# A bidirectional gated scan: the two halves of a head's outputs change places

## The chip, the core and the metric

The kernel runs on one core of one Trainium2 chip. The core has engines that run side by side, each through its own list of instructions in order: TensorE (PE in the profile; its weight loads are PEld), VectorE (DVE), ScalarE (ACT), GpSimd (POOL) and SyncE (SP), which issues most of the DMAs. They meet through semaphores. The metric is the device time of one execution in microseconds (us), the median of the runs.

## What is computed

One layer of an encoder over 1024 positions of width 1024. A normed input is projected by one wide matrix; part of the result goes through a convolution module, part through a bidirectional linear recurrence with 8 heads of width 128, and both are gated and merged; a feed-forward network with a short convolution follows. The change concerns the recurrence (`_bi_hgrn2`). Per head and direction:

```python
# S_t = diag(f_t) S_{t-1} + k_t v_t^T,  o_t = S_t^T q_t
o_fwd = _chunk_gated_scan(qh, heads(k_f), vh, heads(lf_f))
flip = lambda t: jnp.flip(t, axis=1)
o_bwd = flip(_chunk_gated_scan(flip(qh), flip(heads(k_b)), flip(vh), flip(heads(lf_b))))
return o_fwd + o_bwd
...
of = o * lax.rsqrt(jnp.mean(o * o, axis=-1, keepdims=True) + EPS)
of = of.reshape(o.shape[0], o.shape[1], HGRN_WIDTH) * norm_w.astype(jnp.float32)
bmix = (of * jax.nn.silu(og.astype(jnp.float32))).astype(h.dtype)
```

So the outputs of a position need a forward state, summed from the left, and a backward state, summed from the right.

## The kernel before

The kernel keeps TensorE supplied through four stages: the projection, the scan of the heads, the merge, and the feed-forward network. Most products are made of three matmuls in a split format (lines 150 to 152, `mm3`). TensorE's order is the order of the program text (`manual_schedule`). On the other engines a planner orders the instructions by what is ready and by their place in the text, except where the text pins them.

**The scan stage.** The sequence of 1024 is two halves of 512; a half is four chunks of 128. The loop at line 1493 runs over the 8 heads and, inside, over the halves; step `i = 2h + half`. Each step has five places, numbered 0 to 4, at which `between(n)` puts in other work: dense matmuls of the remaining projection columns and of the convolution module (`dense.fill(FILL)`, 1.77 pieces on average, a piece being two of a job's k-steps, six matmuls), then one piece of the previous head's outputs (`pending.fill(1)`), then a step of a base that is prepared ahead (`ahead` at places 0 to 3, `following` at place 4). A head's outputs are therefore made while the first half of the next head is under way, and its final scaling and transposes while the second half is.

**What a step makes.** `scan_base` (line 1241) doubles keys and queries level by level on VectorE, with interleaving copies on ScalarE; its pages are `kG` (3 buffers) and `qF` (4 buffers). `scan_levels` (line 1294) makes a score matrix per chunk: it copies it to `S` and lets GpSimd patch the diagonal blocks by four DMAs (line 1343). `scan_states` (line 1346) transposes the keys (line 1354) and makes the state updates: the forward states `Sf` are chained on VectorE at once (lines 1370 and 1372); the backward ones are only copied, to `Sb` (lines 1382 and 1384), since they need the chunks to their right.

**What the outputs make.** `outputs` (line 1459) first chains the backward states on VectorE, six dependent instructions for chunks 5, 4, 3, 2, 1, 0 (line 1463); chunks 4 to 7 are the second half, in the tile `Sb[1]`, chunks 0 to 3 the first, in `Sb[0]`. After a `yield`, that is one place later, `scan_outputs` (line 1387) makes a half's outputs: per chunk up to three matmuls (line 1405) into the PSUM bank `ob`, of which there is one, then ScalarE copies the bank to a page `on` (line 1407), takes four sums of squares (line 1410), and SP loads the gate (line 1415). One more place later comes the other half, and then the statistic `rs` for both on GpSimd (lines 576 and 577). In the places after that ScalarE scales the two halves (line 1424), and TensorE transposes them for VectorE to gate (line 1434).

A chunk's matmuls read `S`, `v`, the half's `qF` page, `Sf` of the chunk and `Sb` of the chunk. Pages with few buffers are handed on: the base of step `i + 4` takes the `qF` page of step `i`. For the last head there is no next head to run beside; there the places are spelled out (`TAIL`, lines 1528 to 1530), with one dense piece between the two halves' outputs.

Of the kernel before, what the change touches and what calls it, by code (L numbers as in the profile page):

```python
# [49 lines left out]
def tile_hybrid_encoder(  # L50
# [45 lines left out]
    def nm(s):  # L96
        uid[0] += 1
        return f"{s}_{uid[0]}"
# [3 lines left out]
    def bank(tag):  # L102
        return ps.tile([P, H], F32, tag=tag, name=nm(tag), bufs=BANKS[tag])

    def page(pool, tag, bufs, dt=F32):
        return pool.tile([P, H], dt, tag=tag, name=nm(tag), bufs=bufs)

    def tmp():
        return page(mp, "tm", 4)

    def ev():
        return page(mp, "ev", 3)

    def hx():
        return page(mp, "hx", 32, F32R)
# [9 lines left out]
    def split(hi, lo, src, eng, late=False):  # L125
        parts = A.copy(hi, src), eng.tensor_tensor(lo, src, hi.bitcast(F32), op=ALU.subtract)  # L126
        if late:
            for i in parts:
                pin(i)
        return hi, lo  # L130
# [399 lines left out]
    def vec(key, i):  # L530
        name, o = vec_off[key]
        return vecs[name][:, o + i : o + i + 1]
# [41 lines left out]
    def rstd_small(dst, ss, n, late=False):  # L574
        hold = pin if late else lambda i: i
        hold(G.tensor_scalar(dst, ss, 1.0 / n, EPS, op0=ALU.mult, op1=ALU.add))
        hold(G.tensor_tensor(dst, dst, mhalf.to_broadcast(list(dst.shape)), op=ALU.pow))
# [583 lines left out]
    hp = tc.alloc_tile_pool(name="heads", bufs=1, reuse_waits="tile")  # L1161
# [225 lines left out]
    def scan_outputs(h, kept, Sf, Sb):  # L1387


        ons, gates = [], []  # L1390
        ss = cp.tile([P, 2, 4], F32, name=nm("oss"), tag="oss", bufs=2)
        rs = cp.tile([P, 2, 4], F32, name=nm("ors"), tag="ors", bufs=2)
        for half in range(2):
            S_t, v, qF = kept[half]
            o = bank("ob")
            for c in range(4):
                sl = slice(c * P, (c + 1) * P)
                g = half * 4 + c
                terms = [(S_t[:, c, :], v[:, c, :])]
                if g > 0:  # L1400
                    terms.append((qF[:, 1, sl], Sf[half][:, c, :]))
                if g < 7:
                    terms.append((qF[:, 0, sl], Sb[half][:, c, :]))
                for n, (l, r) in enumerate(terms):
                    T.matmul(o[:, sl], l, r, start=(n == 0), stop=(n == len(terms) - 1))  # L1405
            on = tmp()
            A.copy(on, o)
            for c in range(4):
                junk = hp.tile([P, DK], F32, tag="jk", name=nm("jk"), bufs=1)
                A.activation(  # L1410
                    junk, on[:, c * P : (c + 1) * P], AF.Square, accum_out=ss[:, half, c : c + 1]
                )
            ons.append(on)
            gates.append(page(hp, "og", 2))
            nc.sync.dma_start(gates[half], d_og[h][half])
            if half == 0:
                yield
        rstd_small(rs, ss, DK)
        yield
        yield  # L1420
        for half in range(2):
            for c in range(4):
                sl = slice(c * P, (c + 1) * P)
                done = A.activation(
                    ons[half][:, sl], ons[half][:, sl], AF.Copy, scale=rs[:, half, c : c + 1]
                )
            last_scaled[:] = [done]
            yield
        for half in range(2):
            b = bank("tr")  # L1430
            for c in range(4):
                T.transpose(b[:, c * P : (c + 1) * P], ons[half][:, c * P : (c + 1) * P], ident)
            bt = ev()
            V.scalar_tensor_tensor(bt, b, vec("hn", h), gates[half], op0=ALU.mult, op1=ALU.mult)
            if h == NH - 1:
                bm[h][half] = split(hx(), hx(), bt, V)
            else:
                nc.sync.dma_start(d_bm[h][half], bt)
            yield
# [19 lines left out]
    def outputs(h, kept, Tt, Sf, Sb):  # L1459
        for c in range(5, -1, -1):  # L1460
            hf, cc = c // 4, c % 4
            n1, c1 = (c + 1) // 4, (c + 1) % 4
            V.scalar_tensor_tensor(
                Sb[hf][:, cc, :],
                Sb[n1][:, c1, :],
                Tt[:, n1, 1, c1 : c1 + 1],
                Sb[hf][:, cc, :],
                op0=ALU.mult,
                op1=ALU.add,
            )  # L1470
        yield
        yield from scan_outputs(h, kept, Sf, Sb)
# [626 lines left out]
```

## Time and profile before

| | |
|---|---|
| median of 3 runs | 1715.56 us |
| lowest and highest | 1714.04 and 1716.18 us |
| the profiled execution | 1714.14 us |
| its span, first to last instruction | 1712.0 us |
| mean granted TensorE clock | 0.998 |

A row of a view of groups has the line, the engine, the operation and the tiles written and read, then the count and times. A row of a timeline has the start in us from the start of the span, the duration in us, then the engine, line, operation, tiles and shapes; `x2` says that two instructions were merged, and brackets hold the time that the engine stood idle before and what ended it. A row of waits says which engine waited at which line, for which line of which engine, and for how long in total, how often, and at most. The scan lies between about 505 and 860 us of the span. In these stretches, one per head, the engines' busy time in us (windows of the trace; heads' outputs are made in the stretch after their own):

```text
555.00:599.00 44.00, 42.23 (x698) 36.14 (x697) 37.19 (x81) 32.35 (x75) 6.28 (x10) 1.00 0.44 137
599.00:642.00 43.00, 43.00 (x702) 37.11 (x701) 36.55 (x78) 32.89 (x76) 6.51 (x10) 1.00 0.40 128
642.00:686.00 44.00, 43.45 (x702) 37.20 (x700) 37.90 (x85) 32.12 (x75) 6.29 (x10) 1.00 0.42 130
```

The columns are the stretch, its length, then PE, PEld, DVE, ACT and POOL with their counts, the granted clock, the share of the DMA engines and GB/s.

### The profile page before, as it was taken

The page shows a single profiled execution, that of the slowest core. Times are in us where ns is not written, and L with a number is a line of the kernel's source. Part 1 is how long each engine was busy: PE and PEld are TensorE (multiplying, and loading weights), DVE is VectorE, ACT ScalarE, POOL GpSimd, SP SyncE. Part 2 cuts the span into 40 slices and gives each one's busy share as a digit, 9 for nine tenths or more (in the row PEclk, how much of TensorE's full clock was granted, in tenths as well). Part 3 has the DMA queues.
Part 4 walks back from the last instruction along what each step waited for, and adds up shares of the span by engine and source line. Part 5 has one row for each costly group of instructions (what it writes and reads, how often), then busy time and mean ns, then how long its engine had stood idle before and what let it go on. Part 6 is the DMA issues. An engine that isn't in the chain of part 4 may idle for free.

```text
span 1712.0 us, 30393 instructions
## 1 busy us (share of the span) xinstructions
PE 1691.4 (99%) x11719; PEld 1407.6 (82%) x11719; DVE 1263.8 (74%) x1938; ACT 826.2 (48%) x1562; POOL 241.9 (14%) x281
## 2 busy tenths in 40 slices
PE   8999999999999999999999999999999999999998
PEld 6788888888888888888888888888888888888787
DVE  5899999545778888888656467677777776657865
ACT  7444343334666777776432245444344434542334
POOL 1312222200001111111100002122222222000110
PEclk9999999999999999999999999999999999999999
DMA  7887888854673444436788355677777776773852
GB/s 240 279 215 181 191 195 197 208 157 143 223 242 100 137 128 134 128 116 214 233 280 260 123 172 178 151 163 154 166 164 176 171 173 150 236 264 100 214 98 99
DMA packets 332870, 306.16 MB, mean 179 GB/s; under 512 B 17454, under 2 KB 244918, under 8 KB 332726
## 3 DMA queue, kind: packets, MB, share of 16 engines
q1 hardware_dynamic: 285366, 265.42, 48.5%
q0 software_dynamic: 47360, 38.81, 15.5%
q8 instruction: 92, 1.51, 0.4%
q14 instruction: 52, 0.43, 0.1%
HBM read 201.40 MB, written 84.93 MB: 167 GB/s over the span
## 4 chain that ended last, share of the span: by engine, by line
PE 87%; DVE 4%; ACT 2%; DMA 2%; issue 1%; SPq 0%; POOL 0%; POOLq 0%; ACTq 0%; DVEq 0%
PE mm L150 20%; PE mm L152 19%; PE mm L151 19%; PE sc L150 5%; PE sc L151 5%; PE sc L152 5%; PE tr L150 2%; PE tr L151 2%; PE tr L152 2%; PE ob L1405 2%; PE sc L1219 1%; DVE qF L1166 1%; DVE kG L1166 1%; PE sc L1364 1%; PE mm L1364 1%
## 5 line engine op out<-in xcount | busy, mean ns | idle before, releaser
L150 PE MATMUL mm<-hx,wp 128*128 128x512 f32 x1068 | 426.0, 399 | 0.5 <-DVE ev L825 0.4
L152 PE MATMUL mm<-hx,wp 128*128 128x512 f32 x1068 | 417.1, 391 | 0.5 <-DVE wp L126 0.5
L151 PE MATMUL mm<-hx,wp 128*128 128x512 f32 x1068 | 416.2, 390 | 0.6 <-POOL hx L126 0.6
L126 ACT CAST wp<-wr 128x1024 fp32r<-128x1024 f32 (+2 forms) x146 | 146.7, 1005 | 210.6 <-PE mm L151 160.8
L152 PEld LDWEIGHTS mm<-hx,wp 128*128 128x128 f32 x1068 | 200.5, 188 | 44.8 <-DVE wp L126 1.6
L150 PEld LDWEIGHTS mm<-hx,wp 128*128 128x128 f32 x1068 | 200.5, 188 | 42.4 <-DVE ev L825 2.0
L151 PEld LDWEIGHTS mm<-hx,wp 128*128 128x128 f32 x1068 | 200.8, 188 | 39.9 <-POOL hx L126 1.0
L126 DVE TENSOR_TENSOR wp<-wr,wp 128x1024 fp32r<-128x1024 f32 (+2 forms) x144 | 169.4, 1177 | 34.8 <-ACT wp L126 34.5
L1061 DVE SCALAR_TENSOR_TENSOR acc<-gl,v_b,acc 128x1024 f32<-128x1024 f32 x120 | 148.7, 1275 | 0.3
L442 ACT COPY su<-mm 128x512 f32<-128x512 f32 x82 | 47.7, 582 | 83.0 <-PE mm L152 82.6
L1343 POOL DMA_DIRECT2D S<-D x64 | 36.0, 569 | 282.7 <-ACT S L1341 154.2
L1166 DVE TENSOR_TENSOR qF<-qF,tb 128x512 f32<-128x512 f32 x96 | 65.8, 686 | 13.0 <-ACT A L1200 12.3
L126 ACT CAST wq<-sw 128x1024 fp32r<-128x1024 f32 x41 | 43.2, 1054 | 62.2 <-PE mm L151 31.8
L150 PE MATMUL tr<-hx,wp 128*128 128x512 f32 x180 | 70.1, 390 | 0.0
L152 PE MATMUL tr<-hx,wp 128*128 128x512 f32 x180 | 70.1, 389 | 0.0
L151 PE MATMUL tr<-hx,wp 128*128 128x512 f32 x180 | 70.0, 389 | 0.0
L1682 DVE SCALAR_TENSOR_TENSOR tm<-gp,v_a,tm 128x512 f32<-128x512 f32 x88 | 66.0, 750 | 4.1 <-ACT tm L1680 2.0
L1166 DVE TENSOR_TENSOR kG<-kG,tb 128x512 f32<-128x512 f32 x96 | 65.8, 687 | 4.0 <-ACT A L1200 2.3
L303 POOL DMA_DIRECT2D sw<-in_ffn_w_up_dram x38 | 49.8, 1505 | 121.1 <-DMA sw<-in_ffn_w_up_dram 77.8
L150 PE MATMUL sc<-hy,wq 128*128 128x512 f32 x164 | 64.2, 391 | 0.0
L152 PE MATMUL sc<-hy,wq 128*128 128x512 f32 x164 | 63.8, 389 | 0.0
L151 PE MATMUL sc<-hy,wq 128*128 128x512 f32 x164 | 63.8, 389 | 0.0
(378 smaller groups left out, 3716.6 us busy)
## 6 DMA issues: line engine op xcount, KB each, us to landing
wr<-in_w_in_dram SPq DMA_DIRECT2D x48, 512.0 KB, 5.9
wr<-in_ffn_w_up_dram SPq DMA_DIRECT2D x22, 512.0 KB, 5.0
sw<-in_w_in_dram SPq DMA_DIRECT2D x38, 256.0 KB, 3.4
d_g<-ft SPq DMA_DIRECT2D x38, 256.0 KB, 2.0
sw<-in_ffn_w_up_dram SPq DMA_DIRECT2D x38, 256.0 KB, 3.3
sw<-in_ffn_w_up_dram POOLq DMA_DIRECT2D x38, 256.0 KB, 6.8
wr<-sw POOLq DMA_DIRECT2D x32, 256.0 KB, 3.2
wr<-wr POOLq DMA_DIRECT2D x32, 256.0 KB, 3.3
```

Source lines behind the costliest of these rows:

```text
L126: parts = A.copy(hi, src), eng.tensor_tensor(lo, src, hi.bitcast(F32), op=ALU.subtract)
L150: T.matmul(acc, whi[:, k, :], ahi, start=first, stop=False, skip_group_check=again)
L151: T.matmul(acc, whi[:, k, :], alo, start=False, stop=False, skip_group_check=again)
L152: T.matmul(acc, wlo[:, k, :], ahi, start=False, stop=last, skip_group_check=again)
L303: G.dma_start(o, a, accum_op=ALU.add)
L442: A.copy(t, acc)
L1061: V.scalar_tensor_tensor(acc, g[:, k : k + S], tap(k), acc, op0=ALU.mult, op1=ALU.add)
L1166: return V.tensor_tensor(o, a, b, op=op)
L1343: G.dma_start(S_t[g : g + 32, :, g : g + 32], D_t[g : g + 32])
L1364: T.matmul(u[:, sl], kTs[d][:, sl], v[:, c, :], start=True, stop=True)
L1405: T.matmul(o[:, sl], l, r, start=(n == 0), stop=(n == len(terms) - 1))
L1682: V.scalar_tensor_tensor(c, g[:, o + k : o + k + H], vec("fdw", k * NF + j), c, op0=ALU.mult, op1=ALU.add,)
```

## The change

The two halves are computed in the other order: the second half's outputs at the first of the two places, the first half's one place later. The two lists are indexed by half instead of appended to, so that everything after them finds the halves as before; the `yield` between the two follows the half that now comes first. The chain of backward states, the statistic, the scaling and the transposes stay where they are and in their order. Each half issues what it issued before: its matmuls, ScalarE's copy and squares, and one gate load.

```diff
-        ons, gates = [], []
+        ons, gates = [None, None], [None, None]
...
-        for half in range(2):
+        for half in (1, 0):
             S_t, v, qF = kept[half]
...
-            ons.append(on)
-            gates.append(page(hp, "og", 2))
+            ons[half] = on
+            gates[half] = page(hp, "og", 2)
             nc.sync.dma_start(gates[half], d_og[h][half])
-            if half == 0:
+            if half == 1:
                 yield
```

## The prediction

> **What bounds the kernel now.** I read the page first: which engine is full?
>
> ```profile
> span 1712.0 us, 30393 instructions
> ...
> PE 1691.4 (99%) x11719; PEld 1407.6 (82%) x11719; DVE 1263.8 (74%) x1938; ACT 826.2 (48%) x1562; POOL 241.9 (14%) x281
> ```
>
> TensorE (PE) is busy in 1691.4 of 1712.0 us, in an order that the program writes out by hand. So only two things shorten the kernel: less PE work, or fewer stalls of PE, of which the whole span holds 20.6 us. The change adds and removes no instruction, so the question is what it does to stalls. The second view is who PE waited for within the scan (505 to 870 us): the waiting engine and line, the line waited for, then us in total, times, and the longest.
>
> ```profile
> PE ob L1405 <- DVE Sb L1463: 3.2, 4, 1.0
> PE tr L1354 <- DVE kG L1166: 1.3, 2, 1.0
> PE sc L1219 <- ACT A L1200: 0.6, 1, 0.6
> ```
>
> The largest stall of the scan is at the change's own line: in four of the eight heads the output matmuls (L1405) wait for VectorE's chain of backward states (L1463). The timeline of PE shows the place, with start, duration and line; first a head that does not wait (head 0), then head 1, which does, then the waiting rows of heads 3, 5 and 7.
>
> ```profile
> 553.28 0.39 PE L1405 MATMUL ob<-v,S 128*128 128x128 f32 x2
> 553.50 0.39 PE L1405 MATMUL ob<-Sb,qF 128*128 128x128 f32 x2
> 553.73 0.39 PE L1405 MATMUL ob<-v,S 128*128 128x128 f32 x2
> ```
>
> ```profile
> 595.98 0.38 PE L1405 MATMUL ob<-v,S 128*128 128x128 f32 x2
> 597.10 0.49 PE L1405 MATMUL ob<-Sb,qF 128*128 128x128 f32 x2 [0.73 <-DVE Sb L1463]
> 597.42 0.39 PE L1405 MATMUL ob<-v,S 128*128 128x128 f32 x2
> ```
>
> ```profile
> 683.59 0.49 PE L1405 MATMUL ob<-Sb,qF 128*128 128x128 f32 x2 [0.55 <-DVE Sb L1463]
> ...
> 770.41 0.49 PE L1405 MATMUL ob<-Sb,qF 128*128 128x128 f32 x2 [0.99 <-DVE Sb L1463]
> ...
> 851.53 0.49 PE L1405 MATMUL ob<-Sb,qF 128*128 128x128 f32 x2 [0.91 <-DVE Sb L1463]
> ```
>
> **What a stall costs.** Matmuls overlap in the pipe, so the idle gap understates the loss. From one `ob<-v,S` pair to the next takes 553.73 - 553.28 = 0.45 us without a stall and 597.42 - 595.98 = 1.44 us with one: 0.99 us lost, 0.26 more than the 0.73 us of idle that the row shows in brackets. The four rows show 0.73 + 0.55 + 0.99 + 0.91 = 3.18 us; with 0.26 on each, 3.18 + 1.04 = **4.2 us** (1.0, 0.8, 1.25 and 1.2).
>
> **What the change takes away.** The chain has six instructions: c = 5 and 4 write the second half's states (`Sb[1]`), c = 3 to 0 the first half's (`Sb[0]`). The kernel before asks for the first half first, so PE waits for all six. In the new order the first place computes the second half, which reads `Sb[1]` alone: PE waits for two. VectorE's timeline has the second and the last link in head 1, and the second link in heads 3, 5 and 7.
>
> ```profile
> 590.78 0.34 DVE L1463 SCALAR_TENSOR_TENSOR Sb<-Sb,Tt 128x128 f32<-128x128 f32 x1
> ...
> 596.70 0.34 DVE L1463 SCALAR_TENSOR_TENSOR Sb<-Sb,Tt 128x128 f32<-128x128 f32 x1
> ```
>
> ```profile
> 679.99 0.34 DVE L1463 SCALAR_TENSOR_TENSOR Sb<-Sb,Tt 128x128 f32<-128x128 f32 x1
> ...
> 765.09 0.34 DVE L1463 SCALAR_TENSOR_TENSOR Sb<-Sb,Tt 128x128 f32<-128x128 f32 x1
> ...
> 847.68 0.35 DVE L1463 SCALAR_TENSOR_TENSOR Sb<-Sb,Tt 128x128 f32<-128x128 f32 x1
> ```
>
> The second link ends at 591.1, 680.3, 765.4 and 848.0. PE's stalls end at 597.1, 683.6, 770.4 and 851.5, and it arrives 0.8 to 1.25 us before that: the link is done at least 2 us before PE asks. The first place no longer waits for the chain. The second place, which now needs all six links, comes later: in head 1 it ends at 606.9 (a row below) and takes no longer than the first, 599.6 - 596.0 = 3.6 us, so it begins over 6 us after the last link's end at 597.0. In head 7 the two places are closest:
>
> ```profile
> 850.24 0.39 PE L1405 MATMUL ob<-v,S 128*128 128x128 f32 x2
> ...
> 855.26 0.38 PE L1405 MATMUL ob<-v,S 128*128 128x128 f32 x2
> ```
>
> Without the stall the second one begins some 1.2 us earlier, at 854.0, and the chain is done by 851.5, when PE goes on today. Nothing of the wait reappears there. **Term: -4.2 us.**
>
> **What the second half needs earlier than before.** It is read one place sooner, after its `S` has been patched by GpSimd's DMAs (L1343). The last head is the tightest: PE reaches the first place at 850.
>
> ```profile
> 838.71 2.24 POOL L1343 DMA_DIRECT2D S<-D  x4 [10.67 <-ACT S L1341]
> ```
>
> ```profile
> DMA to landing us min/median/max: 1.7/2.6/4.0
> ```
>
> Issue ends at 840.95, and even the longest landing gives 845: 5 us spare. `Sf[1]` is finished on VectorE before the chain starts; `v` is older than both. Cost 0. The gate loads (L1415) swap order in SP's queue, same number and size, and their buffers were last read several places before. The squares, the statistic and the scaling run over the same tiles, and the statistic still waits for whichever half comes second. Cost 0, hidden behind PE's dense pieces; without that cover a swapped gate load would cost one landing, but nothing reads a gate until the next half's transposes.
>
> **What the first half holds longer.** Its `qF` page is given back one place later, and four pages serve `qF`. VectorE opens a new base in that very page (`qF<-q,f`), well ahead of its place in the program. In head 1 and, as the last of six, head 5, that write and the last output matmul of the second place stand so:
>
> ```profile
> 605.42 0.67 DVE L1166 TENSOR_TENSOR qF<-q,f 128x512 f32<-128x512 f32 x1
> ```
>
> ```profile
> 606.52 0.39 PE L1405 MATMUL ob<-Sf,qF 128*128 128x128 f32 x2
> ```
>
> ```profile
> 778.74 0.67 DVE L1166 TENSOR_TENSOR qF<-q,f 128x512 f32<-128x512 f32 x1
> ```
>
> ```profile
> 779.85 0.39 PE L1405 MATMUL ob<-Sf,qF 128*128 128x128 f32 x2
> ```
>
> and in head 3:
>
> ```profile
> 693.00 0.69 DVE L1166 TENSOR_TENSOR qF<-q,f 128x512 f32<-128x512 f32 x1
> ```
>
> ```profile
> 693.00 0.39 PE L1405 MATMUL ob<-Sf,qF 128*128 128x128 f32 x2
> ```
>
> Today the page is free when the first place ends, at about 599.6 (ScalarE's copy of its result starts then, a row below). After the change it is free at 606.9: a **new wait** of 606.9 - 605.4 = 1.5 us on VectorE, and the same in head 5. Four of the six heads with such a write stand like this, head 3 at 0.4 us, head 4 at less: 4 x 1.5 + 0.4 = 6.4 us in all. Queued behind it are the rest of that base's first step, the totals, and the `Sf` updates (L1370, L1372). Who waits for those? VectorE itself runs dry right after:
>
> ```profile
> 611.34 0.29 DVE L1370 COPY Sf<-sc 128x128 f32<-128x128 f32 x1 [0.54 <-PE sc L1364]
> ...
> 615.83 1.23 DVE L126 TENSOR_TENSOR wp<-wr,wp 128x1024 fp32r<-128x1024 f32 x1 [3.05 <-ACT wp L126]
> ```
>
> It idles 0.54 + 3.05 = 3.6 us within the next 11, waiting for PE and ScalarE. A delay of 1.5 us dies there before PE needs a result of it: the `Sf` written then is read a head later. The planner may also put the ready additions (`A<-kG`, `A<-q,f`, 0.68 us each) ahead of the write. Bounds: 0, and 6.4 us if every wait reaches PE. I take 0, the value the idle rows are nearest to.
>
> **What is late next.** With PE 1 us earlier, ScalarE's copy of the outputs and VectorE's next doubling must come earlier too.
>
> ```profile
> 599.63 0.59 ACT L1407 COPY tm<-ob 128x512 f32<-128x512 f32 x1 [2.87 <-PE ob L1405]
> ```
>
> ```profile
> 600.77 0.69 DVE L1166 TENSOR_TENSOR qF<-qF,tb 128x512 f32<-128x512 f32 x1 [1.96 <-ACT A L1200]
> ```
>
> Both can: ScalarE stood 2.87 us waiting for these very matmuls, and VectorE 1.96 us for ScalarE. Their work is paced by PE here and moves with it.
>
> One more price is due to waits of a new kind, and the row comes first:
>
> ```profile
> L1405 PEldq EVENT_SEMAPHORE  x39: 51/51/1566, 549.6 to 852.7; - x39
> ```
>
> The second place may now need one more such instruction per head, 8 x 0.051 = 0.4 us if nothing covered it. But head 0 has them too, and its matmuls keep a pitch of 0.22 us. I count 0. The Trainium skill (Perfetto Trace Analysis, section Identifying Dependency Chains) says that instructions waiting on several engines may get EventSemaphore instructions in front; were each one paid for, the gain would be 3.8 instead of 4.2 us. By that rule, the trace agrees that they are there, not that they cost.
>
> **The sum.** The profiled execution took 1714.14 us (2.1 us outside its span), so the change gives 1714.14 - 4.2 = 1709.9. The three runs' median, 1715.56, lies 1.4 above that execution, so the forecast is 1715.56 - 4.2 = **1711.3 us**.
>
> **The rivals.**
> 1. *The wait moves on.* PE arrives earlier and half of the gain is handed back at the next dependency: the stalls at L1354 and L1219 (1.9 us idle now) grow. For it: VectorE is the second busiest engine of the scan. Against: the idle rows above. 1715.56 - 2.1 = 1713.5.
> 2. *It does not do what it says.* The orders on VectorE and ScalarE come from a planner; if it pushes the first two links back behind other work, the first place waits as before. Against: the smallest margin is 2 us, three rows' worth of VectorE work. 1715.6.
> 3. *Slower: the held `qF` page.* If VectorE's 6.4 us come before its idle and not instead of it, PE pays them at L1354 and at the next levels: -4.2 + 6.4 = +2.2, 1717.8. It decides once the wait per head passes the 3.6 us of idle that follow, or if the planner gives PE something from behind the blocked write. Were VectorE so late that the next half pays it again, -4.2 + 12.8 = +8.6, up to 1724.2.
> 4. *More goes.* The planner's new order also removes the three stalls at L1354 and L1219, 1.3 + 0.6 + 3 x 0.26 = 2.7 us: 1708.6.
>
> **How the numbers follow.** Chances: forecast 0.50 (own range 1710.3 to 1712.3, half the runs' spread either way), rival 1 0.20, rival 2 0.12, rival 3 0.13 with its tail, rival 4 0.05. About 0.2%, 3.4 us, is what a measurement of this kernel can tell from no change: faster means under 1712.1. Of the forecast 0.42 lies there, of rival 1 0.03, rival 4 whole: 0.50. Slower means over 1719.0, the tail of rival 3: 0.08 of its 0.13. The same: 0.42. The range 1709.5 to 1716.0 leaves out rival 4 and rival 3.
>
> **What would show it.** In the new profile PE should have no wait for L1463 at L1405, the first place should start its matmuls at a steady 0.22 us pitch in all eight heads, and the end of head 7's outputs should come about 4 us earlier. VectorE should show a wait for L1405 at `qF<-q,f`, followed by less idle. The forecast is wrong if PE's idle total stays near 20.6 us, or if L1354 rows show new waits for `kG`.

## The result, and the profile after

| | before | after |
|---|---|---|
| median of the comparison, 12 runs each | 1715.54 us | 1710.79 us |
| lowest and highest | 1712.84 and 1717.66 us | 1709.26 and 1713.48 us |
| the profiled execution | 1714.14 us | 1712.07 us |
| its span | 1712.0 us | 1710.1 us |

The ratio of after to before is 0.9974, with a 95% interval of 0.9967 to 0.9982. In time that is 4.75 us less by the medians, and by the interval 1715.54 x 0.0018 = 3.1 to 1715.54 x 0.0033 = 5.7 us. The change is faster, by a quarter of a per cent.

First the page of after: the span and the busy time of each engine.

```profile
span 1710.1 us, 30406 instructions
...
PE 1692.0 (99%) x11719; PEld 1408.3 (82%) x11719; DVE 1263.7 (74%) x1938; ACT 825.1 (48%) x1562; POOL 241.8 (14%) x281
```

Work is as before: the 13 instructions more are all semaphore instructions (GpSimd has 14 more at its DMAs of L1343, others a few less). PE's idle time is 1710.1 - 1692.0 = 18.1 us, where it was 20.6. The view of waits of after, PE in the scan (505 to 870 us), is now complete in two rows:

```profile
PE tr L1354 <- DVE kG L1166: 1.3, 2, 1.1
PE sc L1219 <- ACT A L1200: 0.5, 1, 0.5
```

The row with 3.2 us for the chain (L1463) is gone, and the other two are as they were. The reader should see both halves of that: a wait went, and none grew.

The span got only 1.9 us shorter, less than the gain that the medians show. Where is the rest? The view of line 1405 gives the place: duration, then first and last start of each kind of output matmul, and at the end how long ScalarE waited for these matmuls. Before:

```profile
L1405 PE MATMUL ob<-v,S x128: 270/275/275, 553.3 to 857.4; 128*128 128x128 f32 x128
...
L1405 PE MATMUL ob<-Sf,qF x112: 275/275/275, 553.9 to 857.6; 128*128 128x128 f32 x112
...
  ACT tm L1407: 27.2, 15
```

and after:

```profile
L1405 PE MATMUL ob<-v,S x128: 272/275/276, 555.7 to 855.4; 128*128 128x128 f32 x128
...
L1405 PE MATMUL ob<-Sb,qF x112: 275/275/276, 556.1 to 855.8; 128*128 128x128 f32 x112
L1405 PEldq EVENT_SEMAPHORE  x40: 51/51/1512, 552.0 to 850.9; - x40
...
  ACT tm L1407: 23.1, 14
```

From the first output matmul to the last it was 857.6 - 553.3 = 304.3 us, and is now 855.8 - 555.7 = 300.1: **4.2 us less**. But this execution reached its first output 2.4 us later, before any instruction that the change touches. One row of the waits of PE over the whole span names half of it, 1.2 us, all of it in the projection; first before, then after.

```profile
PE mm L150 <- DVE ev L825: 0.4, 1, 0.4
```

```profile
PE mm L150 <- DVE ev L825: 1.6, 3, 0.7
```

The instructions there stand in the same order in both kernels, so these are differences between executions. A profile of one execution can carry 2 us of them, half of what was looked for; the stretch of the trace that the change touches does not.

The order of instructions says more. From the first to the last, VectorE, ScalarE and GpSimd work through the same list in the same order in both traces (semaphore instructions left out). So the planner chose nothing anew on these engines; what was turned round is PE's order of the two halves and, with it, what the copies and loads behind them work on.

Now head 1, at the place where the kernel before lost 0.99 us. The timeline of PE of after, first place:

```profile
598.46 0.38 PE L1405 MATMUL ob<-v,S 128*128 128x128 f32 x2
598.67 0.39 PE L1405 MATMUL ob<-Sf,qF 128*128 128x128 f32 x2
598.90 0.39 PE L1405 MATMUL ob<-Sb,qF 128*128 128x128 f32 x2
599.12 0.39 PE L1405 MATMUL ob<-v,S 128*128 128x128 f32 x2
```

From one `ob<-v,S` pair to the next it takes 0.66 us: three products at 0.22 and no gap. It is so in every head: the 22 output matmuls of the first place start within 2.34 to 2.35 us in all eight heads now. In the trace of before they took 3.33, 3.16, 3.60 and 3.52 us in heads 1, 3, 5 and 7, so the four stalls lost 0.99, 0.82, 1.26 and 1.18 us, 4.25 us in sum. The timeline of VectorE of after has the chain's second and last link, and further on two rows of bases:

```profile
593.21 0.34 DVE L1463 SCALAR_TENSOR_TENSOR Sb<-Sb,Tt 128x128 f32<-128x128 f32 x1
...
599.14 0.34 DVE L1463 SCALAR_TENSOR_TENSOR Sb<-Sb,Tt 128x128 f32<-128x128 f32 x1
...
602.24 0.69 DVE L1166 TENSOR_TENSOR qF<-qF,tb 128x512 f32<-128x512 f32 x1 [0.98 <-ACT A L1200]
...
606.89 0.67 DVE L1166 TENSOR_TENSOR qF<-q,f 128x512 f32<-128x512 f32 x1
```

The chain is as late as ever: its last link ends at 599.5, a microsecond after PE has begun the outputs. PE simply no longer asks for it. The link that it does ask for ended at 593.55, 4.9 us before the place. ScalarE's copy of the result, in its own timeline, has lost a microsecond of waiting, 1.90 us where it was 2.87:

```profile
601.11 0.59 ACT L1407 COPY tm<-ob 128x512 f32<-128x512 f32 x1 [1.90 <-PE ob L1405]
```

VectorE's doubling after it waits 0.98 us where it was 1.96. Over the scan, ScalarE's wait for the output matmuls falls from 27.2 to 23.1 us (the two views of line 1405 above). The engines that PE paces gave up idle time, nothing else.

### The profile page after: what moved, and what is told of

It reads as the page before. It is cut to its first block, busy times and chain, and to the rows that moved or that the text cites. A ratio compares the mean times of both kernels' runs of the same rounds, so it can differ in the third digit from the quotient of the medians.

```text
span 1710.1 us, 30406 instructions
## 1 busy us (share of the span) xinstructions
PE 1692.0 (99%) x11719; PEld 1408.3 (82%) x11719; DVE 1263.7 (74%) x1938; ACT 825.1 (48%) x1562; POOL 241.8 (14%) x281
## 4 chain that ended last, share of the span: by engine, by line
PE 86%; DVE 4%; DMA 2%; ACT 2%; issue 1%; POOL 0%; SPq 0%; POOLq 0%; ACTq 0%; DVEq 0%
PE mm L150 20%; PE mm L152 19%; PE mm L151 19%; PE sc L150 4%; PE sc L152 4%; PE sc L151 4%; PE ob L1405 2%; PE tr L150 2%; PE tr L151 2%; PE tr L152 2%; DVE acc L1061 2%; PE sc L1219 1%; PE sc L1305 1%; DMA d_cv<-acc 1%; PE mm L1364 1%
## 5 line engine op out<-in xcount | busy, mean ns | idle before, releaser
L152 PE MATMUL mm<-hx,wp 128*128 128x512 f32 x1068 | 417.1, 391 | 0.5 <-DVE wp L126 0.5
L152 PEld LDWEIGHTS mm<-hx,wp 128*128 128x128 f32 x1068 | 200.5, 188 | 44.7 <-DVE wp L126 1.4
L1343 POOL DMA_DIRECT2D S<-D x64 | 36.0, 569 | 278.6 <-ACT jk L1410 125.5
L152 PE MATMUL tr<-hx,wp 128*128 128x512 f32 x180 | 70.1, 389 | 0.0
L150 PE MATMUL sc<-hy,wq 128*128 128x512 f32 x164 | 64.2, 392 | 0.0
L152 PE MATMUL sc<-hy,wq 128*128 128x512 f32 x164 | 63.8, 389 | 0.0
L150 PE MATMUL mm<-hy,wp 128*128 128x512 f32 x164 | 63.8, 389 | 0.0
```

The source lines that it names most:

```text
L150: T.matmul(acc, whi[:, k, :], ahi, start=first, stop=False, skip_group_check=again)
L152: T.matmul(acc, wlo[:, k, :], ahi, start=False, stop=last, skip_group_check=again)
L1343: G.dma_start(S_t[g : g + 32, :, g : g + 32], D_t[g : g + 32])
```

## The experiments

The theory: the whole gain is PE's four waits for the chain in heads 1, 3, 5 and 7. Rivals: the new order helps elsewhere too (other orders on VectorE, pages freed at other times), or any escape from the wait is given back further on. Each kernel has five rounds beside the kernel before on the same chip; the kernel before had a median of 1715.36 us over the first five experiments and 1714.9 over the last four. Diffs are against the kernel before unless the text says otherwise; the list indexing of the change is left out of them.

**The new order in the odd heads only.**

```diff
-        for half in range(2):
+        for half in ((0, 1), (1, 0))[h % 2]:
...
-            if half == 0:
+            if half == h % 2:
                 yield
```

> The new order in heads 1, 3, 5 and 7 alone, which are the four heads whose output matmuls waited for the chain of backward states; the other four keep the old order. Theory (the gain is PE's four waits and nothing else): the whole gain is here, 4.2 us less than before in the scan (from the first to the last output matmul 304.1 - 4.2 = 299.9 us), no wait of L1405 for L1463, and about 4.2 to 4.7 us less in all (1711 us). Rival (the gain comes from pages and queues that are freed in another order, in every head): half of it, 2.1 to 2.4 us.

Measured: 1710.38 us, ratio 0.9971 (0.996 to 0.9982). Waits of PE in the scan:

```profile
PE tr L1354 <- DVE kG L1166: 1.3, 2, 1.1
...
```

and no row for L1463. From the first to the last output matmul it took 853.5 - 553.4 = 300.1 us, where 299.9 was expected. That is the change's whole gain; the interval, 3.1 to 6.9 us, leaves out the rival's 2.1 to 2.4.

**The new order in the even heads only.** The same edit with `((1, 0), (0, 1))[h % 2]` and `if half == 1 - h % 2`.

> The new order in heads 0, 2, 4 and 6 alone, which did not wait. Theory: nothing, 304.1 us from the first to the last output matmul, the four waits of 3.2 us in sum unchanged, the time within the noise of before (1715.5 us). Rival (pages and queues, in every head): 2.1 to 2.4 us less.

Measured: 1715.33 us, ratio 0.9998 (0.9989 to 1.0007). Waits of PE in the scan:

```profile
PE ob L1405 <- DVE Sb L1463: 3.2, 4, 1.0
...
```

All four waits are there, the stretch is 858.3 - 553.9 = 304.4 us (304.1 was expected), and no time is gained; the interval allows at most 1.9 us, just under the rival's 2.1. The gain sits in the odd heads, where the waits were, and turning the halves round has no merit of its own that can be measured.

**Another cure: the first half's chunks from right to left.** The halves stay in the old order; the chunk whose state is chained last is taken last.

```diff
-            for c in range(4):
+            for c in (range(4) if half else range(3, -1, -1)):
                 sl = slice(c * P, (c + 1) * P)
                 g = half * 4 + c
```

> The old order of the halves, but the four chunks of the first half are taken from the right (3, 2, 1, 0), as the chain makes them. If PE's wait is for a chunk's own state, the first chunk needs three links and the fourth, some 1.9 us later, all six: in heads 1, 3, 5 and 7 the stalls shrink from 4.2 to 1 us or less, so the time falls by 3 to 4 us without any swap of the halves. If the wait goes with the whole tile of the half's states, or if the gain of the change was not this wait, nothing: 1715.5 us and 3.2 us of waits.

Measured: 1711.34 us, ratio 0.9975 (0.9966 to 0.9985), and no wait for L1463; the stretch of the outputs is 856.7 - 556.5 = 300.2 us, as in the change. In head 1, the backward products of chunks 3, 2, 1 and 0 in the timeline of PE:

```profile
599.69 0.39 PE L1405 MATMUL ob<-Sb,qF 128*128 128x128 f32 x2
...
600.36 0.39 PE L1405 MATMUL ob<-Sb,qF 128*128 128x128 f32 x2
...
601.03 0.39 PE L1405 MATMUL ob<-Sb,qF 128*128 128x128 f32 x2
...
601.48 0.39 PE L1405 MATMUL ob<-Sb,qF 128*128 128x128 f32 x2
```

and the links for the same chunks in that of VectorE:

```profile
597.36 0.33 DVE L1463 SCALAR_TENSOR_TENSOR Sb<-Sb,Tt,Sb 128x128 f32<-128x128 f32 x1
...
598.22 0.33 DVE L1463 SCALAR_TENSOR_TENSOR Sb<-Sb,Tt 128x128 f32<-128x128 f32 x1
...
599.09 0.33 DVE L1463 SCALAR_TENSOR_TENSOR Sb<-Sb,Tt 128x128 f32<-128x128 f32 x1
...
599.95 0.33 DVE L1463 SCALAR_TENSOR_TENSOR Sb<-Sb,Tt 128x128 f32<-128x128 f32 x1
```

Each chunk's link ends 2.0, 1.8, 1.6 and 1.2 us before its product starts. The last link ends at 600.28, after PE has begun the place and long before it gets to chunk 0. So PE waits for the chunk that it reads, not for the whole tile, and the old order asked for the last link first. In this kernel, too, the other engines keep their order of instructions. A cure that leaves the halves and the order in which they release their pages as they were has the same gain: what the halves' order does to pages is worth nothing that can be measured.

**Give the chain more time: both halves one place later, in the old order** (heads 0 to 6; the scaling stays where it was).

```diff
-        yield
+        yield from [None] * (1 + (h < NH - 1))
         yield from scan_outputs(h, kept, Sf, Sb)
...
         rstd_small(rs, ss, DK)
-        yield
+        yield from [None] * (h == NH - 1)
         yield
```

> The old order of the halves, both of them one place later in heads 0 to 6 (one of the two empty places after the statistic is moved ahead of them); the last head as before. The chain then has a whole place more, so heads 1, 3 and 5 lose their waits (1.0 + 0.8 + 1.25 = 3.05 us) and head 7 keeps its own (1.2 us): theory 3 us less, 1712.5 us. Both halves now hold their page of queries over the moment at which VectorE opens the base after next. Rival (the held page): VectorE waits up to 1.5 us per head, and if that reaches PE, up to 6.4 us come back: -3 + 6.4 = +3.4, 1719 us, with new waits of L1354 or L1219 for VectorE. If VectorE's other work only moves ahead of the blocked write, nothing comes back.

Measured: 1715.21 us, ratio 1.0 (0.9991 to 1.0009): neither. Waits of PE in the scan:

```profile
PE tr L1354 <- DVE kG L1166: 3.2, 3, 1.6
PE sc L1219 <- issue: 1.1, 1, 1.1
PE ob L1405 <- DVE Sb L1463: 1.0, 1, 1.0
PE sc L1219 <- ACT A L1200: 0.5, 1, 0.5
```

The chain's waits fell to head 7's, which this edit leaves alone. But the wait at the key transposes (L1354) grew from 1.3 to 3.2 us, and 1.1 us came in at L1219. The four rows sum to 5.8 us; before, the three sum to 5.1. The wait has moved on, whole, as in the prediction's first rival, but not because PE arrives earlier. The trace shows another way. The outputs come a place later while their scaling stays where it was, so ScalarE now stands waiting for the statistic and then does all eight scalings in a row; before, the scalings stood among other work. In head 0, in the timelines of ScalarE, VectorE and PE:

```profile
572.17 2.45 ACT L1424 ACTIVATE tm<-tm,ors 128x128 f32<-128x128 f32 x8 [2.27 <-POOL ors L577]
```

```profile
575.19 0.69 DVE L1166 TENSOR_TENSOR qF<-qF,tb 128x512 f32<-128x512 f32 x1 [2.96 <-ACT A L1200]
```

```profile
582.86 0.55 PE L1354 MATMUL tr<-ident,kG 128*128 128x128 f32 x3 [1.65 <-DVE kG L1166]
```

The interleaving copies (L1200) stand behind the scalings, VectorE's doubling waits for such a copy, and the keys reach PE 0.6 us later than before, when VectorE's longest wait from 571 to 581 us was 1.37 us and PE's wait here 1.04. Heads 2 and 4 show the same block of eight scalings with such a wait of VectorE behind it (3.34 and 2.76 us). That is read from the trace; no kernel here spreads the scalings again to test it.

**The held page.** The prediction expected the base's write of `qF` to wait for the half that comes second. It had not done so (head 1, above). Here, with the change in place, the second half's page is held as well: a small matmul before the last chunk of the second place reads it, and its result is overwritten at once.

```diff
-                g = half * 4 + c
+                g = half * 4 + c; g == 3 and T.matmul(o[:, 3 * P : 3 * P + 32], kept[1][2][:, 1, sl], Sf[1][:, 3, :32], start=True, stop=True)
```

> The changed kernel, with one small matmul added in the second place of each head (before the last chunk; its result is overwritten) that reads the second half's page of queries once more, so that this page is held until some 2 us into the second place. Theory: in the changed kernel the base after next opens in the page of the half that comes first, which is free by then, so VectorE has no new wait; holding it makes the planner put two or three ready instructions ahead of the blocked write, and PE pays little: 1711 to 1712 us, at most 1 us over the changed kernel. Rival (the prediction's third: a held page reaches PE): waits of L1354 or L1219 for VectorE grow by 2 to 6 us, 1713 to 1717 us.

Measured: 1712.37 us, ratio 0.9985 (0.9977 to 0.9994). In head 1 the timeline of PE, from the end of chunk 2 to chunk 3, with the added pair on line 1398:

```profile
604.99 0.39 PE L1405 MATMUL ob<-Sb,qF 128*128 128x128 f32 x2
605.22 0.31 PE L1398 MATMUL ob<-Sf,qF 128*128 128x32 f32 x2
605.36 0.47 PE L1405 MATMUL ob<-v,S 128*128 128x128 f32 x2
605.66 0.39 PE L1405 MATMUL ob<-Sf,qF 128*128 128x128 f32 x2
```

and that of VectorE:

```profile
604.25 0.67 DVE L1166 TENSOR_TENSOR tb<-f 128x512 f32<-128x512 f32 x1
604.84 0.68 DVE L1166 TENSOR_TENSOR A<-kG 128x512 f32<-128x512 f32 x1
605.44 0.68 DVE L1166 TENSOR_TENSOR A<-q,f 128x512 f32<-128x512 f32 x1
606.04 0.68 DVE L1166 TENSOR_TENSOR qF<-q,f 128x512 f32<-128x512 f32 x1
```

The write now comes only after the added matmul, and three instructions that were ready stand ahead of it; VectorE does not idle, and no row of its waits in the scan names the output matmuls. In the change itself the write stood where it did before, so holding this page is what moved it: in the change the base does open in the second half's page, which is free first. The write comes 2.6 us after the place has begun (603.43) instead of 1.1, so it is put off by the very 1.5 us that the prediction had feared. What the kernel lost against the change is the added matmul: from `ob<-Sb,qF` to the second product after it, `ob<-Sf,qF`, it takes 0.67 us instead of 2 x 0.22, so 0.22 to 0.23 us a head, 1.8 us in eight. The stretch of the outputs grew by as much, from 300.1 to 854.7 - 552.9 = 301.8 us, and the ratios differ by 0.0011 x 1715 = 1.9 us (over the bound of 1 us that was expected, which had not counted the matmul). PE's waits did not grow (1.0 us at L1354, 0.5 at L1219). Holding the page this long cost PE nothing that can be measured.

**The later outputs with a fifth page.** The kernel with both halves one place later, and `qF` with five buffers.

```diff
-        qF = hp.tile([P, 2, H], F32, tag="qF", name=nm("qF"), bufs=4)
+        qF = hp.tile([P, 2, H], F32, tag="qF", name=nm("qF"), bufs=5)
```

> The kernel with both halves one place later in the old order, as before, but with five pages of queries instead of four, so that no base waits for a page. That kernel gained nothing, though three of the four waits for the chain were gone: new waits at L1354 (3.2 us for 1.3) and L1219 took their place. If the held page was their cause: they go back to 1.9 us, and the time falls by 3 us against before, to 1712.4 us. If it is the later copies and squares on ScalarE that run into the next step's work: the waits stay, 1715 us.

Measured: 1713.51 us, ratio 0.9991 (0.9982 to 1.0). Waits of PE in the scan:

```profile
PE tr L1354 <- DVE kG L1166: 3.5, 3, 1.4
PE ob L1405 <- DVE Sb L1463: 0.4, 1, 0.4
PE sc L1219 <- issue: 0.3, 1, 0.3
```

The wait for the keys stayed, at 3.5 us, so the page is not its cause. The little that was gained, 1.5 us by the ratio and not clear of nothing, goes with the smaller rows of L1463 and L1219. ScalarE's blocks of eight scalings are here as well. One other suspect for the late keys was tried:

**The change, with the transposes and the gating one place later** (heads 0 to 6; diff against the change).

```diff
             last_scaled[:] = [done]
-            yield
+            yield from [None] * (1 + (half == 1 and h < NH - 1))
```

> The changed kernel with the transposes of both halves one place later (heads 0 to 6), so that VectorE's two gating instructions (L1434, 0.74 us each) no longer stand ahead of the keys for which PE waits at L1354 in heads 1 and 4. If those gatings are what delays the keys: the 1.3 us of waits at L1354 go, 1.5 to 1.8 us less than the changed kernel, 1709 us. If not, the same as the changed kernel, 1710.8 us, or slower where they now meet other work.

Measured: 1714.17 us, ratio 0.9998 (0.9989 to 1.0006). Waits of PE over the whole span:

```profile
PE mm L152 <- DVE wp L126: 2.5, 2, 2.0
...
PE tr L1354 <- DVE kG L1166: 1.7, 3, 1.1
PE sc L1219 <- ACT A L1200: 1.0, 1, 1.0
```

The keys' wait grows only by 0.4 us: gating later is not enough to hold them up as the later outputs did. The gain is lost in another way in this execution: half a microsecond at L1219, and a wait of 2.0 us for a weight (L152) at 872.8 us, after the scan, where the change waited 0.5 us at that line in all. What delays the keys when the outputs come later stays open; the block of scalings is what the traces point to.

**Is there more in the chain?** The change, with the last four links one place later (diff against the change).

```diff
     def outputs(h, kept, Tt, Sf, Sb):
         for c in range(5, -1, -1):
+            if c == 3:
+                yield
...
-        yield
         yield from scan_outputs(h, kept, Sf, Sb)
```

> The changed kernel with the chain's last four links given to the planner one place later, since only the first two are needed by the first place. PE has no wait left there, so the theory gives 0 in most heads; where the second place follows closely (heads 4 and 7, 3.3 us after the first), the last link may now be late: 0 to 1.5 us slower, 1711 to 1712 us. A gain of 1 to 2 us would mean that the early links hold up the doublings for which PE waits at L1354 and L1219.

Measured: 1710.05 us, ratio 0.9975 (0.9965 to 0.9985), as the change. Waits of PE in the scan:

```profile
PE tr L1354 <- DVE kG L1166: 1.4, 2, 1.1
PE sc L1219 <- ACT A L1200: 0.6, 1, 0.6
```

VectorE gets 1.4 us of work out of the way of its doublings, and PE has no use for it: no wait of the change's scan hangs on the chain, and the stretch of the outputs is 852.4 - 552.4 = 300.0 us, as in the change. No version clearly beats the change.

## Why the prediction was right, and where it failed

The forecast was 1711.3 us, and 1710.79 was measured, inside the range; the forecast case, not a rival, is what happened.

- **What is removed.** Right. The four waits are gone in the trace. Turned in the odd heads alone, where the waits were, the order gives the whole gain; turned in the even heads alone, it gives none.
- **What a stall costs.** Right, and it mattered. Idle time alone would have given 3.2 us. The allowance of 0.26 us for each stall, read in head 1 alone, made it 4.2. It holds in all four: the first places lost 4.25 us in sum, and from first to last output matmul the trace lost 4.2. The medians' 4.75 (3.1 to 5.7) agrees with both, so it is the trace that tells them apart.
- **The second link is in time, and the second place does not wait.** Right: the second link ends 2.3 to 7.4 us before the first place in the eight heads of after (4.9 in head 1), the last link 3.0 us or more before the second place, and there is no row for L1463. The trace of before also says why the other heads were spared: in heads 2 and 6 the last link ended only 0.5 and 0.2 us before PE began.
- **The held `qF` page.** This step failed, though the cost that was taken, 0, came out. The prediction put it that VectorE "opens a new base in that very page" and would wait 1.5 us in head 1. It read which page the base takes from one order and carried it over to the other. The base takes the page that is given back first. In the new order that is the second half's, at the end of the first place, so the write stands 1.1 us into the second place (606.89; that place starts at 605.77, rows below) with no wait at all. In all six heads with such a write it starts before the last output matmul of the second place has ended. So the rule given with the kernel before, that the base of step `i + 4` takes the page of step `i`, holds for the old order of the halves only. The slower rival, which rested on this wait, had lost its ground before any hiding by idle time came into play. That the cost of 0 came out for this step in the change was luck, since there was no wait to hide. Of the two escapes that the prediction named for a held page, page_held shows the second: ready additions were put ahead of the write, and no wait of VectorE for it is left to see.

The timeline of PE of after, first and last pair of the second place in head 1, while the write at 606.89 is under way:

```profile
605.77 0.39 PE L1405 MATMUL ob<-v,S 128*128 128x128 f32 x2
...
608.00 0.39 PE L1405 MATMUL ob<-Sb,qF 128*128 128x128 f32 x2
```

- **What else is held.** The prediction looked at `qF` alone. `S` and `v` have three buffers each, and the first half's are given back one place later too. It cost nothing that shows: ScalarE's waits at their lines (L1341 and L1518) are 2.1 and 3.4 us in after, 2.1 and 3.3 before, and none of them is for L1405.
- **Work that PE paces moves along.** Right: the waits of ScalarE and VectorE behind PE shrank by what PE gained.
- **The extra semaphore instructions.** Costed at 0, rightly, but at L1405 there is one more (40 for 39), not one per head.
- **"The end of head 7's outputs about 4 us earlier."** On the clock of the span it came 1.8 us earlier (857.6 to 855.8), since this execution entered the scan 2.4 us late. Measured from the first output it is 4.2.
- **The rivals.** "The wait moves on" did not happen here. With both halves one place later a wait did move on and took all that three heads' waits should have given, though not by the rival's mechanism: as far as the trace shows, it went through ScalarE. "It does not do what it says" did not happen: the planner kept the order of VectorE, ScalarE and GpSimd. "More goes" did not happen: the waits at L1354 and L1219 stayed to 0.1 us.

## What to carry to other kernels

Where a consumer waits for a serial chain, look which link each piece of it reads, and take the pieces in the order in which the chain delivers them: here that cost no time on any engine, while starting the consumer later may only move the wait. Count a stall of pipelined matmuls from start to start, not by the idle gap, and compare kernels over the stretch that the edit touches when the whole run varies by half of the effect. Where pages are handed on, an edit that changes the order of release also changes who takes which page; the old trace does not show that pairing.

## What was not expected of the hardware

A pair of matmuls with a quarter of the columns was no cheaper here. In page_held the added pair with 32 columns left PE after 0.14 us (605.22 to 605.36), but the full pair behind it then took 0.30 instead of 0.22, so the two together cost as much as two full ones. The weight loads point to why. In both pairs they are of 128 columns, and from the short pair's loads to those of the next pair it is 0.22 us, as between full pairs.

```profile
605.11 0.30 PEld L1398 LDWEIGHTS ob<-Sf,qF 128*128 128x128 f32 x2
605.33 0.30 PEld L1405 LDWEIGHTS ob<-v,S 128*128 128x128 f32 x2
```

And a stage whose instructions stand in the same order can vary by more than a microsecond between executions: in the projection PE's waits for L825 were 0.4 us before, 1.6 us after, and in the kernel with turned chunks, in the view of waits over its whole span:

```profile
PE mm L150 <- DVE ev L825: 2.4, 2, 2.1
```
